# Turning the tests of an expert's rows, so that its arms stand short, middle, long in the program

## The chip, the cores and the metric

The kernel runs on one core of a Trainium2 chip. The metric is device time in microseconds (us), the median of three runs. The engines are PE (TensorE, matmuls; PEld is its weight load), DVE (VectorE), ACT (ScalarE), POOL (GpSimd) and SP (SyncE, which here issues the weight transfers). Each engine runs its own instruction stream, branches included.

## The reference, cut to what matters

Two transformer blocks are computed over 256 tokens of 1024 features. The first has a mixture of experts: 32 experts, each token goes to its four best. Cut from the reference:

```python
logits = (xt @ w_router).astype(jnp.float32) + b_router.astype(jnp.float32)
top_v, top_i = lax.top_k(logits, TOP_K)
gates = jax.nn.softmax(top_v, axis=-1)
...
def expert_block(args):
    xb, e = args
    hdn = xb @ w_gate_up[e] + b_gate_up[e]
    return clamped_swiglu(hdn) @ w_down[e] + b_down[e]
...
out = jnp.zeros((T, D), y.dtype).at[tok_sorted].add(y[dest] * g_sorted[:, None].astype(y.dtype))
```

How many tokens an expert gets is known only at run time. In these inputs 21 experts get up to 32, 8 get 33 to 64, and 3 get more.

## The kernel before

**Stages.** Up to about 201 us the kernel does the first block's attention and routing. From there to about 1195 us come the experts, and then the rest of the two blocks. All changes are in the experts' part.

**Weights.** Each expert has 12 slabs of 1 MB (eight of gate and up, four of down). The class Stream issues them on SP's queue (L192) into a ring of buffers, in the order in which they are used. A slab's buffer is free again when PE has done the last matmul that reads it; a transfer whose buffer isn't free waits on SP, and all later ones wait behind it.

**Arms.** For each expert the program holds several versions of the work, one for each class of row count n, and every engine branches to one of them: the few arm (n up to 32, functions few_up and few_down), the narrow arm (33 to 64, narrow_up and narrow_down) and the mid arm (over 64, mid_up and mid_down), with two wide passes ahead of it for more than 96 and 224 rows, which these inputs never take. An arm begins on PE with two bias matmuls (L1041), then come eight slabs of gate and up (L1028, with a weight tile of 128x32 in a few and 128x64 in a narrow arm; mid begins likewise but also gathers its rows, L1162), the preparation of the next expert's rows, and the down slabs (L1106 in few, L1036 in narrow, L1225 in mid). Its last step, rows_out, takes the result from PSUM into the tile Y with two copies on ACT (L1047) and two subtractions on DVE (L1050). Few and narrow arms read Y only at their middle, when combine adds the expert before; a mid arm needs DVE before its first matmul.

**The order of the arms.** The list of experts is unrolled: 32 times the tests, the long passes, mid, narrow, few, one behind the other, and then a join. The tests of an expert are L1344 (few or not), L1345 (narrow or not) and L1346 (wide or not). An arm that isn't last ends with a jump over the arms behind it to the join (shown at L1345 behind narrow); the last one runs on into the join. At the join PE loads the next count (L1324) and makes the next expert's tests. name_jump, at each arm's start, looks at the next expert's count (L1333) and gives PE a hint which of the next tests will be taken; the hint is an instruction of PE alone.

The times of the steps below are read from the trace. Experts are numbered from 0. The order that the counts give is: narrow 0, few 1, 2, narrow 3, 4, few 5, narrow 6, few 7, 8, mid 9, few 10, narrow 11, 12, mid 13, few 14 to 18, narrow 19, mid 20, few 21 to 24, narrow 25, few 26 to 31.

Of the kernel before, what the change touches and what calls it, by code (L numbers as in the profile page):

```python
# [96 lines left out]
def kernel(tc, a, out, taps=None, stop=None):  # L97
# [848 lines left out]
    def early_loads():  # L946
        nc.gpsimd.dma_start(gt_f, row(bt[1][:], D, 1024))
        load_gn(0)
        nc.gpsimd.dma_start(cols, a["cols"])
# [23 lines left out]
    def mask(e):  # L973
        for t in range(2):
            mask_rows(dm, t, e)
        slab_rows(e)
# [54 lines left out]
    def down(yb, hT, base, kk):  # L1031
        w = W.get(base + 8 + DS[kk // 2])
        j, c = divmod(kk, 4)
        for hf in range(2):
            o = (kk % 2) * 1024 + hf * 512
            nc.tensor.matmul(yb[64 * hf:64 * hf + 64, :], hT[:, c, j * 64:(j + 1) * 64], w[:, o:o + 512],  # L1036
                             start=(kk == KK[0]), stop=(kk == KK[-1]), skip_group_check=True,
                             tile_position=(0, 64 * hf))
# [13 lines left out]
    def combine(y, dT):  # L1052
        for t in range(2):
            for hf in range(2):
                nc.tensor.matmul(acc[t][:, hf * 512:hf * 512 + 512], dT[:, t, :], y[:, hf, :], start=False,
                                 stop=False, skip_group_check=True)
# [255 lines left out]
    def whole(up, down, e):  # L1312

        up(e)
        d = None
        if e:
            combine(Y, PRE[e - 1][1])
        if e + 1 < NE:
            mask(e + 1)
            d = dm  # L1320
        down(e, d, Y)

    def load_n(e):
        return nc.values_load(cnt[0:1, e:e + 1], min_val=0, max_val=T)  # L1324

    def name_jump(e, n):

        def likely(label):
            tc.mark_branch_hint_location(f"{label}{e}", "LikelyTaken", [mybir.EngineType.PE])

        if n is None:
            return
        with tc.If(n > 32) as c:  # L1333
            with tc.If(n > 64) as d:
                likely("wide")
            with d.Else():
                likely("narrow")
        with c.Else():
            likely("few")

    n = load_n(0)
    for e in range(NE):
        nn = load_n(e + 1) if e + 1 < NE else None
        with tc.If(n > 32, label=f"few{e}") as cmp:  # L1344
            with tc.If(n > 64, label=f"narrow{e}") as many:  # L1345
                with tc.If(n > 96, label=f"wide{e}"):  # L1346
                    wide(e, 96)
                    with tc.If(n > 224):
                        wide(e, 224)
                name_jump(e + 1, nn)  # L1350
                whole(mid_up, mid_down, e)
            with many.Else():
                name_jump(e + 1, nn)
                whole(narrow_up, narrow_down, e)
        with cmp.Else():
            name_jump(e + 1, nn)
            whole(few_up, few_down, e)
        for k in range(12):
            W.done(MOE0 + 12 * e + k)
        if e == 1:  # L1360
            early_loads()
        n = nn
# [606 lines left out]
```

## Time and profile before

| | before |
|---|---|
| median of three runs | 2091.35 us (2090.78 to 2092.16) |
| profiled execution, its own time | 2093.27 us |
| its span | 2091.5 us |
| mean granted clock of PE | 0.93 |
| PE busy | 1804.8 us (86%) |
| DVE, ACT, POOL busy | 45%, 32%, 18% |
| weights moved on SP's queue | 586.72 MB |

The span is what the trace covers; the profiled execution's time is 1.8 us longer. Shares over the whole span mix three stages. In the experts' part two things can set the pace: the stream of slabs, when PE sits waiting for a transfer, and PE, when the ring is full and the transfers wait for PE. Which of the two holds at a place is seen in the rate of the DMA engines there.

### The profile page before, as it was taken

To read this page: it belongs to the slowest core of one execution; us is meant where nothing else is said; L and a number is where in the kernel's file an instruction comes from. 1 tells how busy PE (TensorE), PEld (TensorE's weight loads), DVE (VectorE), ACT (ScalarE), POOL (GpSimd) and SP (SyncE) were. 2 spreads that over 40 slices of the span, in tenths; PEclk is the share of its full clock that TensorE was granted. 3 is DMA by queue.
4 is the path that set the end of the run, shared out by engine and by line. 5 is a ranking of instruction groups with operands and counts; after the bars stand their busy time and mean duration, and the time that the engine had idled before them with its cause. 6 is when DMAs were issued, how large, how long until landed. Compare 5 with 4: busy or idle time off the path is not lost.

```text
span 2091.5 us, 28801 instructions
## 1 busy us (share of the span) xinstructions
PE 1804.8 (86%) x11311; PEld 1159.1 (55%) x11311; DVE 943.7 (45%) x1687; ACT 674.8 (32%) x1149; POOL 366.6 (18%) x337
## 2 busy tenths in 40 slices
PE   7998898787897877797766688998999989999998
PEld 4775233222322222232221168997998778988996
DVE  3774222212212321131221259857575589665763
ACT  3452111101101110111110145544564456445752
POOL 3323000000000000000000044124352242132640
PEclk9997999998998989898988789999999999999999
DMA  9868999998968999899999853454455533453552
GB/s 399 348 244 305 407 418 418 419 418 357 419 273 331 417 419 418 349 376 420 417 419 418 347 196 109 142 183 171 155 188 213 178 133 134 162 201 131 182 198 84
DMA packets 85796, 602.35 MB, mean 288 GB/s; under 512 B 9888, under 2 KB 10576, under 8 KB 14256
## 3 DMA queue, kind: packets, MB, share of 16 engines
q1 hardware_dynamic: 81600, 586.72, 70.6%
q0 software_dynamic: 3952, 12.53, 2.0%
q8 instruction: 135, 2.21, 0.4%
q14 instruction: 109, 0.89, 0.1%
HBM read 598.13 MB, written 1.08 MB: 287 GB/s over the span
## 4 chain that ended last, share of the span: by engine, by line
issue 49%; PE 35%; DVE 10%; POOL 2%; ACT 2%; POOLq 1%; DVEq 0%; ACTq 0%
PE psum L354 11%; PE psum L353 10%; PE psum L352 10%; DVE lo L325 1%; DVE lx L325 1%; POOL v L245 1%; DVE gl L1740 1%; DVE gl L1524 1%; DVE h L577 1%; PE psum L1674 1%; DVE nm L570 1%; DVE x L285 0%; PE psum L448 0%; ACT hTh L357 0%; POOLq L1324 0%
## 5 line engine op out<-in xcount | busy, mean ns | idle before, releaser
L1028 PE MATMUL psum<-w,xT 128*32 128x512 f32 (+1 forms) x1504 | 268.6, 673 | 54.7 <-DMA w<-in_wgu_dram 52.6
L354 PE MATMUL psum<-hTh,lo 128*128 128x256 f32 x848 | 240.8, 284 | 2.9 <-DVE lo L325 2.9
L352 PE MATMUL psum<-hTh,hi 128*128 128x256 f32 x848 | 242.1, 286 | 0.4 <-DVE yl L1544 0.4
L353 PE MATMUL psum<-hTl,hi 128*128 128x256 f32 x848 | 240.6, 284 | 0.0
L248 POOL TENSOR_TENSOR yr<-v,mhalf 128x1 f32<-128x1 f32 (+1 forms) x26 | 21.0, 808 | 1146.6 <-DVE v L245 1145.3
L325 DVE TENSOR_TENSOR lo<-w,hi 128x2048 fp32r<-128x2048 f32 x84 | 193.7, 2309 | 59.3 <-ACT hi L319 59.3
L319 ACT ACTIVATE hi<-w 128x2048 fp32r<-128x2048 f32 x93 | 177.6, 1913 | 86.5 <-PE psum L354 51.2
L1028 PEld LDWEIGHTS psum<-w,xT 128*32 128x32 f32 (+1 forms) x1504 | 61.9, 125 | 238.7 <-issue 119.6
L1006 DVE TENSOR_SCALAR g<-psum 64x256 f32<-64x256 f32 (+1 forms) x70 | 29.3, 418 | 363.1 <-PE psum L1028 362.4
L1007 ACT ACTIVATE s<-g 64x256 f32<-64x256 f32 (+1 forms) x70 | 28.8, 411 | 474.9 <-DVE g L1006 474.9
L352 PEld LDWEIGHTS psum<-hTh,hi 128*128 128x128 f32 x848 | 162.6, 192 | 3.6 <-issue 2.9
L354 PEld LDWEIGHTS psum<-hTh,lo 128*128 128x128 f32 x848 | 162.5, 192 | 3.3 <-DVE lo L325 3.3
L353 PEld LDWEIGHTS psum<-hTl,hi 128*128 128x128 f32 x848 | 162.5, 192 | 0.0
L1050 DVE TENSOR_TENSOR y<-psum,y 64x512 fp32r<-64x512 f32 x64 | 44.1, 689 | 212.5 <-ACT y L1047 186.1
L1786 POOL TENSOR_TENSOR cv<-cv,cv 128x256 f32<-128x256 f32 x44 | 86.8, 1973 | 135.1 <-ACT cv L1785 135.1
L354 PE MATMUL psum<-hTh,lx 128*128 128x256 f32 x368 | 104.0, 283 | 2.9 <-DVE lx L325 2.9
L352 PE MATMUL psum<-hTh,hx 128*128 128x256 f32 x368 | 104.4, 284 | 0.0
L325 DVE TENSOR_TENSOR lx<-w,hx 128x2048 fp32r<-128x2048 f32 x40 | 92.4, 2310 | 26.3 <-ACT hx L319 26.2
L353 PE MATMUL psum<-hTl,hx 128*128 128x256 f32 x368 | 103.7, 282 | 0.0
L1041 PE MATMUL psum<-bgh,eb 128*128 128x512 f32 x70 | 30.3, 519 | 83.2 <-issue 73.6
L1780 DVE SCALAR_TENSOR_TENSOR cv<-psum,cols,cv 128x255 f32<-128x255 f32 x176 | 72.8, 476 | 61.9 <-ACT cv L1776 61.9
L319 ACT ACTIVATE hx<-w 128x2048 fp32r<-128x2048 f32 x43 | 82.3, 1913 | 38.5 <-PE psum L354 18.4
(427 smaller groups left out, 3759.6 us busy)
## 6 DMA issues: line engine op xcount, KB each, us to landing
w<-in_wgu_dram SPq DMA_DIRECT2D x169, 1024.0 KB, 19.8
w<-in_wpk_dram SPq DMA_DIRECT2D x168, 1024.0 KB, 4.9
w<-in_wd_dram SPq DMA_DIRECT2D x83, 1024.0 KB, 20.0
lo<-in_wgu_dram SPq DMA_DIRECT2D x29, 1024.0 KB, 19.8
hi<-in_wgu_dram SPq DMA_DIRECT2D x28, 1024.0 KB, 19.8
hi<-in_wd_dram SPq DMA_DIRECT2D x16, 1024.0 KB, 20.4
lo<-in_wd_dram SPq DMA_DIRECT2D x15, 1024.0 KB, 20.8
hx<-in_wgu_dram SPq DMA_DIRECT2D x15, 1024.0 KB, 19.9
```

The lines of the kernel that those rows point to most:

```text
L319: nc.scalar.activation(s.his[i], W.get(i), AF.Copy)
L325: (eng or nc.vector).tensor_tensor(s.los[i], W.get(i), s.his[i].bitcast(F32), OP.subtract)
L352: nc.tensor.matmul(o, lh, rh, start=start, stop=False, **k)
L353: nc.tensor.matmul(o, lh, rl, start=False, stop=False, **k)
L354: nc.tensor.matmul(o, ll, rh, start=False, stop=stop, **k)
L1006: nc.vector.tensor_scalar(g, gl[:, c], 7.0, None, op0=OP.min)
L1007: nc.scalar.activation(s, g, AF.Sigmoid, scale=1.702)
L1028: nc.tensor.matmul(b[o:o + n, :], l, w[:, q * 512:q * 512 + 512], start=False, stop=(k == 7), skip_group_check=True, tile_position=(0, o))
L1041: nc.tensor.matmul(b, lhsT, bgh[:, o:o + 512], start=first, stop=False, skip_group_check=True)
L1050: nc.vector.tensor_tensor(y[o, hf, :], yb[r, :], y[r, hf, :].bitcast(F32), OP.subtract)
L1780: nc.vector.scalar_tensor_tensor(cv[q][:, o], bnk[:, q, i], c4[q][:, 2 * d:2 * d + 1], cv[q][:, o], op0=OP.mult, op1=OP.add)
L1786: nc.gpsimd.tensor_tensor(cv[0], cv[0], cv[1], OP.mult)
```

## The change

Both inner tests are written the other way round, and their bodies exchanged with them: first the few arm, else the narrow arm, else the wide passes and mid. The argument preferred_fallthrough_block=False tells the compiler to lay the other body out behind the test, which keeps the long arm where it was.

```diff
--- before.py
+++ after.py
@@ -1341,20 +1341,20 @@
     n = load_n(0)
     for e in range(NE):
         nn = load_n(e + 1) if e + 1 < NE else None
-        with tc.If(n > 32, label=f"few{e}") as cmp:
-            with tc.If(n > 64, label=f"narrow{e}") as many:
+        with tc.If(n < 33, label=f"few{e}", preferred_fallthrough_block=False) as cmp:
+            name_jump(e + 1, nn)
+            whole(few_up, few_down, e)
+        with cmp.Else():
+            with tc.If(n < 65, label=f"narrow{e}", preferred_fallthrough_block=False) as many:
+                name_jump(e + 1, nn)
+                whole(narrow_up, narrow_down, e)
+            with many.Else():
                 with tc.If(n > 96, label=f"wide{e}"):
                     wide(e, 96)
                     with tc.If(n > 224):
                         wide(e, 224)
                 name_jump(e + 1, nn)
                 whole(mid_up, mid_down, e)
-            with many.Else():
-                name_jump(e + 1, nn)
-                whole(narrow_up, narrow_down, e)
-        with cmp.Else():
-            name_jump(e + 1, nn)
-            whole(few_up, few_down, e)
         for k in range(12):
             W.done(MOE0 + 12 * e + k)
         if e == 1:
```

In the built program the number of instructions, their waits and the semaphores are the same on each engine. The tests compare with 33 and 65 in place of 32 and 64, and are now at L1344, L1348 and L1352. Of the places in memory, mid's and the wide passes' are the same. Those of few and narrow are exchanged: in memory an expert's arms were mid, narrow, few, and are mid, few, narrow. On PE both have nearly the same number of instructions, so that the second place and the third are as large as before; only who stands there differs. The rows below are of PE, as the program lists its instructions. In it h is an expert's hidden rows, hT and the numbered xT tiles are the same transposed, xe the next expert's gathered rows, w a slab of weights, cst_85 a constant, and cnt the counts.

The end of the second place in expert 8, and what stands behind it, before:

```order
L998 MATMUL psum<-cst_85,xe 128x128 x4
L1036 MATMUL psum<-w,hT 64x512 x8
L1018 MATMUL psum<-cst_85,h 128x128 x2
L1036 MATMUL psum<-w,hT 64x512 x8
L1345 UNCONDITIONAL_BRANCH
L1333 COMPARE_AND_BRANCH
```

And after the change:

```order
L998 MATMUL psum<-cst_85,xe 128x128 x4
L1106 MATMUL psum<-w,xT_7924 32x512 x8
L1096 MATMUL psum<-cst_85,h 128x64 x2
L1106 MATMUL psum<-w,xT_7924 32x512 x8
L1344 UNCONDITIONAL_BRANCH
L1333 COMPARE_AND_BRANCH
```

The few arm (L1096 and L1106) now stands there, and it now has the end jump (L1344), over the arm behind it.

The end of the third place in expert 11, up to the tests of expert 12, before:

```order
L998 MATMUL psum<-cst_85,xe 128x128 x4
L1106 MATMUL psum<-w,xT_10815 32x512 x8
L1096 MATMUL psum<-cst_85,h 128x64 x2
L1106 MATMUL psum<-w,xT_10815 32x512 x8
L1344 UNCONDITIONAL_BRANCH
L1324 TENSOR_LOAD cnt
L1344 COMPARE_AND_BRANCH
L1345 COMPARE_AND_BRANCH
L1346 COMPARE_AND_BRANCH
```

And after:

```order
L998 MATMUL psum<-cst_85,xe 128x128 x4
L1036 MATMUL psum<-w,hT 64x512 x8
L1018 MATMUL psum<-cst_85,h 128x128 x2
L1036 MATMUL psum<-w,hT 64x512 x8
L1348 UNCONDITIONAL_BRANCH
L1324 TENSOR_LOAD cnt
L1344 COMPARE_AND_BRANCH
L1348 COMPARE_AND_BRANCH
L1352 COMPARE_AND_BRANCH
```

The narrow arm (L1018 and L1036) now stands last. The listing shows an end jump on each last arm; in the built program that jump leads to the next instruction and is left out, so that the last arm runs on into the load of the next count and the tests.

## Rows read from the trace of the kernel before

**Rows 1.** Busy time by stretch: us, five engines, PE clock, DMA share, GB/s.

```profile
605.00:670.00 65.00, 50.49 (x264) 16.43 (x266) 11.22 (x28) 5.83 (x13) 0.00 (x0) 0.84 0.61 231
...
895.00:1164.00 269.00, 206.62 (x1210) 64.55 (x1202) 64.26 (x169) 35.54 (x78) 0.00 (x0) 0.88 1.01 419
```

**Rows 2.** Timeline of PE, starts of arms: start, us, [idle before].

```profile
304.75 0.73 PE L1041 MATMUL psum<-bgh,eb 128*128 128x512 f32 x2 [2.94 <-issue]
...
391.19 1.22 PE L1041 MATMUL psum<-bgh,eb 128*128 128x512 f32 x2 [3.03 <-issue]
...
450.22 0.71 PE L1041 MATMUL psum<-bgh,eb 128*128 128x512 f32 x2 [3.00 <-DVEq L1346]
...
532.83 0.74 PE L1041 MATMUL psum<-bgh,eb 128*128 128x512 f32 x2
...
565.01 1.22 PE L1041 MATMUL psum<-bgh,eb 128*128 128x512 f32 x2 [4.31 <-issue]
...
597.77 0.70 PE L1041 MATMUL psum<-bgh,eb 128*128 128x512 f32 x2 [3.35 <-DVEq L1346]
...
664.01 1.21 PE L1041 MATMUL psum<-bgh,eb 128*128 128x512 f32 x2 [8.60 <-issue]
...
685.51 0.73 PE L1041 MATMUL psum<-bgh,eb 128*128 128x512 f32 x2 [2.50 <-issue]
...
702.90 0.73 PE L1041 MATMUL psum<-bgh,eb 128*128 128x512 f32 x2
...
721.12 0.73 PE L1041 MATMUL psum<-bgh,eb 128*128 128x512 f32 x2
...
757.64 1.22 PE L1041 MATMUL psum<-bgh,eb 128*128 128x512 f32 x2 [5.47 <-issue]
...
782.95 0.73 PE L1041 MATMUL psum<-bgh,eb 128*128 128x512 f32 x2
...
820.42 0.76 PE L1041 MATMUL psum<-bgh,eb 128*128 128x512 f32 x2 [3.24 <-DVEq L1346]
...
889.41 1.21 PE L1041 MATMUL psum<-bgh,eb 128*128 128x512 f32 x2 [8.85 <-issue]
...
1013.74 0.73 PE L1041 MATMUL psum<-bgh,eb 128*128 128x512 f32 x2 [2.90 <-issue]
```

**Rows 3.** Timeline of SP, its first issue behind the second middle arm.

```profile
667.15 0.33 SPq L192 DMA_DIRECT2D lx<-in_wgu_dram  x1
```

**Rows 4.** Branches in PE's sequencer, two lines: ns min/median/max, first and last start.

```profile
L1344 PEldq COMPARE_BRANCH  x32: 74/360/6084, 194.8 to 1162.3; - x32
...
L1346 PEldq COMPARE_BRANCH  x3: 346/5001/5160, 446.1 to 814.7; - x3
```

**Rows 5.** The same between 1005 and 1013.6 us: end jump, then the test.

```profile
L1345 PEldq COMPARE_BRANCH  x1: 335/335/335, 1007.2 to 1007.2; - x1
...
L1344 PEldq COMPARE_BRANCH  x1: 5251/5251/5251, 1008.1 to 1008.1; - x1
```

**Rows 6.** Timeline of DVE ahead of the first two middle arms.

```profile
448.61 1.41 DVE L1050 TENSOR_TENSOR y<-psum,y 64x512 fp32r<-64x512 f32 x2 [6.08 <-ACTq L1346]
...
595.76 1.41 DVE L1050 TENSOR_TENSOR y<-psum,y 64x512 fp32r<-64x512 f32 x2 [9.66 <-ACTq L1346]
```

**Rows 7.** Busy time by stretch, right behind five arm starts.

```profile
391.20:394.60 3.40, 3.40 (x18) 1.10 (x22) 1.28 (x5) 0.00 (x0) 0.00 (x0) 0.55 1.02 412
...
450.20:457.00 6.80, 6.78 (x43) 2.88 (x44) 1.81 (x7) 0.77 (x2) 0.00 (x0) 1.00 1.02 416
...
597.80:606.00 8.20, 8.20 (x38) 3.26 (x40) 1.59 (x7) 0.77 (x2) 0.00 (x0) 0.58 1.01 415
...
820.40:831.00 10.60, 8.80 (x36) 3.56 (x38) 1.75 (x7) 0.77 (x2) 0.00 (x0) 0.52 1.01 413
...
1013.70:1017.10 3.40, 3.36 (x30) 1.21 (x34) 0.00 (x0) 0.00 (x0) 0.00 (x0) 1.00 1.02 412
```

**Rows 8.** Timeline of PE in expert 19, its eighth slab.

```profile
801.99 1.94 PE L1028 MATMUL psum<-hx,xT 128*64 128x512 f32 x8 [0.55 <-DMA hx<-in_wgu_dram]
```


## The prediction

> **What bounds the kernel now.** I read the rates by stretch first. From 895 to 1164 us the transfers run at 419 GB/s with a DMA share of 1.01, so there the stream sets the pace; from 605 to 670 us they fall to 231 GB/s, since the ring is full and waits for PE [rows 1]. The transfers restart at 667.15 us [rows 3], 3.1 us after the few arm behind mid 13 starts at 664.01 [rows 2]; behind mid 20, whose few arm starts at 889.41, it is the same. After a restart the stream runs without a hole up to the next mid arm, and behind mid 20 to the end of the experts. So time lost by PE counts in two places: from the start of mid 9 (450.22) to the few arm at 664.01, and in mid 20, from 820.42 to 889.41. Elsewhere a few arm that doesn't wait takes 702.90 to 721.12, 18.2 us [rows 2], and its 12 slabs of 1.05 MB each take 30 us at 419 GB/s, so some 5 us more hide behind the stream.
>
> Then I read the starts of arms with the idle time ahead of each [rows 2]. Starts behind few are mostly without a gap (532.83, 702.90, 721.12, 782.95); starts behind narrow have 2.90 to 4.31 us. The reason stands in PE's own branches. Behind narrow 25 the end jump takes 0.335 us, and then the test of the next expert takes 5.25 us [rows 5]. This is so behind each of the eight narrow arms (5.00 to 5.46). Behind few the test takes about 0.36 us, the median of the line, in 13 of 20 cases, and 3.1 to 6.1 us in the other seven [rows 4]. The test starts about 1 to 2.5 us ahead of the last matmul's end, since PE's sequencer runs ahead of its queue, and so 5.2 us of test give some 3 to 5 us of gap. I read it thus: the test jumps over the arms ahead of its target, PE has to fetch the code there, and the hint at an arm's start starts that fetch early. Behind the last place, which runs on into the test, the early fetch is still there mostly; behind the second place, whose jump passes over a whole arm, it is not.
>
> The Trainium skill bears on this ("Runtime: NRT & Kernel Launch", Instruction fetch mechanics): prefetch is purely sequential, and a taken branch out of the two pages held has to fetch its target first. By it all far tests would stall, whichever place an arm has, and the change would give nothing. The trace doesn't agree: 13 tests behind few are short [rows 4], in a kernel with hints.
>
> **The change part by part.** The instructions, waits and semaphores are the same, and the tests' other constants cost nothing. What moves is who stands in the second place (jump over one arm) and who in the third (runs on). I take the cost to go with the place, since the jump and the distance belong to it: 20 exits from few with a successor get the full stall, and most of the eight exits from narrow lose it. Most of that hides. On the path are these, in order.
>
> 1. *Few 8 to mid 9.* Before, its test took 0.346 us, the smallest of its line [rows 4], and the gap is 3.00 [rows 2], because mid waits for DVE, which ends at 448.61 + 1.41 = 450.02 [rows 6], 0.2 us ahead of the start. With jump and stall PE's branches end later than that: the gap becomes that of a full stall behind few, 0.33 + 5.1 less the 1.1 us by which the test starts ahead of the matmuls' end, plus 0.7 from test to matmul, so 5.0 (bounds from rows: 4.31 and 5.47). That is +2.0. Behind it the clock, too: right behind the start at 450.22 it is granted 1.00 (2.4 GHz), but behind mids that start after 3.35 and 3.24 us of gap 0.58 over 8.2 us and 0.52 over 10.6 us, which is mostly the lower level, 1.2 GHz [rows 7]. A gap of 5.0 brings that: 8.2 x 0.42 = 3.4 or 10.6 x 0.48 = 5.1, taken +4.3. Sum **+6.3** (+4.7 to +7.6).
> 2. *Few 10 to narrow 11.* Gap 0 at 532.83, then 5.05: +5.05. A narrow arm that starts after a long gap costs more by its clock: 565.01 to 597.77 less the gap of 3.35 is 29.4, 532.83 to 565.01 less 4.31 is 27.9 [rows 2], so +1.5. Sum **+6.6** (+5.8 to +7.0).
> 3. *Narrow 11 to narrow 12.* Narrow now runs on into the test: gap 4.31 to 0, and the slow start goes: **-5.8**.
> 4. *Narrow 12 to mid 13.* The test falls from 5.16 to 0.35, but DVE holds the start: it ends at 595.76 + 1.41 = 597.17 [rows 6], 0.6 us ahead of the start at 597.77, where 0.2 would do. So -0.4, and the gap becomes 2.95. The open question is the clock. Behind narrow a gap of 2.90 kept it at 1.00 and one of 3.03 had 0.55 [rows 2, 7]; behind few 3.00 kept it. I give it a bit less than even odds to stay up, and enter 45% of the 3.4: -1.5. Sum **-1.9** (-3.8 to -0.4).
> 5. *Narrow 19 and mid 20.* Few 14 to 17 get stalls: two starts without gap become 5.05 each, that at 685.51 grows by 2.5, and each loses some 1.5 by the clock, 17 in all. Few 17 lasts 36.5 with a gap of 5.47, 12.8 more than 18.2, and few 18 25.3, 7 more, all of it waiting for slabs; these take it up. Narrow 19 then starts 5.05 later than 782.95, at 788.0. Its eighth slab starts at 801.99 after a wait for its transfer [rows 8]; now 788.0 + 0.7 + 7 x 1.94 + 1.5 for the clock = 803.8, so +1.8. Mid 20's start gains 0.3 as in 4, and its clock 0 to 5.1, taken 45%: -2.3. Sum **-0.8** (-3.6 to +1.5).
>
> The other stalls and gains fall where the stream sets the pace, at nil: few 2, 5 and 7 ahead of mid 9, few 21 to 30 behind mid 20. Without that cover each would cost 5 to 6.5. The last expert's arm has no next test; its jump costs 0.3 and the last combine waits longer for Y. The jump out of mid, and the test behind it, stay as they are.
>
> Together +6.3 + 6.6 - 5.8 - 1.9 - 0.8 = **+4.4 us**. The profiled execution took 2093.27, 1.9 above the median; the sum of differences is put on the median, 2091.35, which gives 2095.7.
>
> **The rivals.**
> - *Clock as before* or *clock won twice.* The same mechanism with the two open clocks at their ends: both mids start slowly again, 2.3 + 1.5 more than the sum, 2099.5; both start at full clock, 2.8 + 1.9 less, 2091.0. Both are within the forecast's case and make its range.
> - *Narrow stalls in the third place, too.* Seven of 20 exits from there did. If narrow 11's does, term 3 goes (+5.8) and the time is about 2101.5. Against it: the narrow arm lasts 28 us to few's 18 with as many instructions, so an early fetch has more time. It decides at one exit.
> - *The stall goes with the arm.* If narrow stalls since of what it does, or few's short test has another reason than its place, or the code lies as before for PE, nothing moves: 2091.4. For it: eight of eight against 13 of 20 is also a split by arm. Against it: seven exits of few stall at times as long, and both arms carry the same hint.
> - *Every far test stalls, whatever its place.* The short tests behind few would then be the odd ones, and no place worse than another: each exit as before, 2091.4. The rule of the Trainium skill named above is this case. Against it the 13 short tests [rows 4]; 0.03.
> - *Few does not stall behind its jump, though narrow loses its stall.* Terms 1 and 2 vanish, and 5's +1.8: -5.8 - 1.9 - 0.3 - 2.3 = -10.3, 2081.1. The faster side. For it: few reaches its jump sooner after its hint, so that what the hint fetched may not yet be displaced. Against it: the jump's target lies as far away as narrow's did.
>
> **How the numbers follow.** A measurement of this kernel tells about 0.2%, 4.2 us, from no change: faster is below 2087.2, slower above 2095.5. The forecast's mechanism has 0.73: with both clocks low 0.22 (2099.5), one low 0.36 (2096.1 with 13's won, 2094.4 with 20's won), both full 0.15 (2091.0). Narrow's stall staying has 0.10 (2101.5), the arm's stall or nothing moved 0.09 (2091.4), every far test alike 0.03 (2091.4), few without a stall 0.05 (2081.1). Slower: 0.22, two thirds of 0.36's first half, a quarter of its second, and most of 0.10, together 0.48. Faster: 0.05 and a little of the case with both clocks full, 0.07. The rest, 0.45, is no change to be told. The range leaves out the case without few's stall and the upper part of narrow's: 2089.5 to 2101.0. The forecast, 2095.7, lies at the edge of what can be told, and slower is the likelier side by little.
>
> **What would show it.** In the profile after, the starts behind few should have gaps near 5 (narrow 11, narrow 19, mid 9), with PE's test behind each few arm at 5.0 to 5.5 and an end jump of about 0.33; the start of narrow 12 should have none, and the mids at 13 and 20 a gap of 2.9 to 3.0 with the test at 0.35. The few arm behind mid 13 should start some 5 later counted from mid 9's place, and the transfers restart 3.1 behind it. Stalls should stand at about 26 of 31 exits, where there were 18. The step is wrong if the tests behind few stay short, if the test behind narrow 11 is long, or if the clock behind mid 9's start stays at 1.00.

## The result, and the profile after

The changed kernel takes 2109.47 us, the median of four runs (2101.28 to 2117.04), against 2091.76 for the kernel before (2090.78 to 2093.32). The ratio is 1.0081 with an interval of 1.0064 to 1.0098: slower by 17.7 us of the medians, less than 1% but clear of the noise. The forecast was 2095.7 with a range up to 2101.0, so the direction was the one held likelier, and the size that was forecast is four times too small, with the time outside the range. The profiled execution took 2101.28, the fastest of the four; a second trace, below, is of a longer one.

These are the starts of arms in the profiled execution, on PE, with the idle time ahead of each in brackets. They answer to [rows 2]; the views are of short windows, which cut a line's duration and count.

```profile
451.96 0.79 PE L1041 MATMUL psum<-bgh,eb 128*128 128x512 f32 x2 [4.96 <-DVE d L1155]
...
543.69 0.80 PE L1041 MATMUL psum<-bgh,eb 128*128 128x512 f32 x1 [5.19 <-issue]
...
573.53 0.73 PE L1041 MATMUL psum<-bgh,eb 128*128 128x512 f32 x2
...
604.35 0.71 PE L1041 MATMUL psum<-bgh,eb 128*128 128x512 f32 x2 [2.95 <-DVEq L1352]
...
667.85 0.79 PE L1041 MATMUL psum<-bgh,eb 128*128 128x512 f32 x1 [9.01 <-issue]
...
695.18 0.79 PE L1041 MATMUL psum<-bgh,eb 128*128 128x512 f32 x1 [8.49 <-issue]
...
718.70 0.79 PE L1041 MATMUL psum<-bgh,eb 128*128 128x512 f32 x1 [4.67 <-issue]
...
742.43 0.69 PE L1041 MATMUL psum<-bgh,eb 128*128 128x512 f32 x1 [4.70 <-issue]
...
775.29 0.80 PE L1041 MATMUL psum<-bgh,eb 128*128 128x512 f32 x1 [10.86 <-issue]
...
803.03 0.79 PE L1041 MATMUL psum<-bgh,eb 128*128 128x512 f32 x1 [7.99 <-issue]
...
835.92 0.70 PE L1041 MATMUL psum<-bgh,eb 128*128 128x512 f32 x2 [2.95 <-DVEq L1352]
```

Mid 9, narrow 11, narrow 12 and mid 13 (the first four) have the gaps that were forecast: 5.0, 5.05, none and 2.95. The few arm behind mid 13 starts 3.8 later than before, where the sum to there was +5.2. What was not forecast are the gaps of 8 to 11 us at 695.18, 775.29 and 803.03, which is behind few 14, few 17 and few 18.

The branches of PE show why. These are the branches at L1344 (end jump of a few arm, and the test for a few arm) and L1348 (test for a narrow arm), in the columns of [rows 4]. The first row is from the end of few 14, with jump and test on one line, the second of few 17 likewise. The third is few 18 (the jump, and a test not taken) and the last two few 10.

```profile
L1344 PEldq COMPARE_BRANCH  x2: 4088/4706/5324, 684.8 to 689.4; - x2
...
L1344 PEldq COMPARE_BRANCH  x2: 5476/5700/5924, 762.6 to 769.0; - x2
...
L1344 PEldq COMPARE_BRANCH  x2: 84/1630/3176, 793.2 to 796.8; - x2
...
L1344 PEldq COMPARE_BRANCH  x2: 84/202/319, 536.6 to 537.4; - x2
L1348 PEldq COMPARE_BRANCH  x1: 5282/5282/5282, 537.6 to 537.6; - x1
```

Behind few 10 it is as forecast: the jump 0.319, the test 5.28. Behind few 14 the jump alone takes 4.09 us, and the test 5.32 on top; behind few 17 the jump takes 5.92 and the test 5.48; behind few 18 the jump takes 3.18. Nine of the 20 exits from few have such a long jump (few 1, 7, 14, 17, 18, 21, 24, 27, 28: 2.9 to 6.1 us), the other eleven have 0.32 to 0.35. Seven of the nine are the very experts whose test was long behind the third place before; the other two, 18 and 28, had a short one.

The granted clock behind the starts of mids 9, 13 and 20, in the columns of [rows 7]:

```profile
452.00:460.00 8.00, 8.00 (x36) 3.22 (x38) 1.33 (x5) 0.54 (x2) 0.00 (x0) 0.57 1.02 418
...
604.30:611.10 6.80, 6.75 (x43) 2.87 (x44) 1.82 (x7) 0.77 (x2) 0.00 (x0) 1.00 1.01 414
835.90:842.70 6.80, 6.78 (x43) 2.90 (x44) 1.81 (x7) 0.77 (x2) 0.00 (x0) 1.00 1.01 413
```

Mid 9 lost its full clock, as forecast, and in this execution mids 13 and 20 both won theirs. The starts on the path, in us from the span's start, for all kernels of this study. The first expert's arm starts at 200.7 to 204.5 in these traces, so that differences within a row tell more than the starts themselves.

| kernel | mid 9 | few 14 | narrow 19 | mid 20 | few 21 | few 14 to narrow 19 |
|---|---|---|---|---|---|---|
| before | 450.2 | 664.0 | 783.0 | 820.4 | 889.4 | 118.9 |
| after | 452.0 | 667.9 | 803.0 | 835.9 | 900.3 | 135.2 |
| after, second trace | 453.6 | 666.6 | 807.3 | 840.5 | 908.5 | 140.7 |
| after, arms laid out early | 453.6 | 672.4 | 796.3 | 829.7 | 897.5 | 123.9 |
| before, arms laid out early | 451.1 | 667.7 | 787.0 | 824.7 | 890.5 | 119.3 |
| after, 14 to 18 in the old order | 454.5 | 674.4 | 794.7 | 831.4 | 894.6 | 120.4 |
| after, early, 8 and 10 in the old order | 452.3 | 658.5 | 782.6 | 816.2 | 881.6 | 124.1 |
| before without hints | 468.5 | 698.2 | 822.0 | 856.4 | 923.1 | 123.8 |
| after, arms laid out late | 486.5 | 727.1 | 879.2 | 913.8 | 983.6 | 152.2 |

In the profiled execution the loss behind few 14 stands in one stretch: from there to narrow 19 it is 16.2 us, of which 4.6 come back in narrow 19, which waited for slabs before, and 4.6 in mid 20 by its clock. So few 21 starts 10.9 later, and the rest of the experts, paced by the slabs, follows: the first matmul behind them starts at 1218.79 where it was 1206.82. Of these 12.0 us 4.0 come back behind the experts, in code that didn't change (why isn't shown), and this execution is 8.0 longer than the profiled one before.

### The profile page after: what moved, and what is told of

It is laid out like the page before. It is cut to its first block, busy times and chain, and to the rows that moved or that the text cites. A ratio compares the mean times of both kernels' runs of the same rounds, so it can differ in the third digit from the quotient of the medians.

```text
span 2099.5 us, 28866 instructions
## 1 busy us (share of the span) xinstructions
PE 1781.8 (85%) x11311; PEld 1159.7 (55%) x11311; DVE 944.3 (45%) x1687; ACT 674.8 (32%) x1149; POOL 366.7 (17%) x337
## 4 chain that ended last, share of the span: by engine, by line
issue 50%; PE 34%; DVE 10%; ACT 2%; POOL 2%; POOLq 1%; DVEq 0%; ACTq 0%
PE psum L354 10%; PE psum L353 10%; PE psum L352 10%; DVE lo L325 1%; DVE lx L325 1%; POOL v L245 1%; DVE gl L1740 1%; DVE h L577 1%; DVE gl L1524 1%; DVE nm L570 1%; DVE x L285 0%; PE psum L1674 0%; ACT hTh L357 0%; POOLq L1324 0%; PE psum L448 0%
## 5 line engine op out<-in xcount | busy, mean ns | idle before, releaser
L1028 PE MATMUL psum<-w,xT 128*32 128x512 f32 (+1 forms) x1504 | 258.1, 660 | 16.3 <-DMA w<-in_wgu_dram 10.6
L1041 PE MATMUL psum<-bgh,eb 128*128 128x512 f32 x70 | 36.7, 618 | 168.8 <-issue 157.9
L1041 PEld LDWEIGHTS psum<-bgh,eb 128*128 128x128 f32 x70 | 15.0, 267 | 199.5 <-issue 199.5
## 6 DMA issues: line engine op xcount, KB each, us to landing
w<-in_wgu_dram SPq DMA_DIRECT2D x169, 1024.0 KB, 19.8
hi<-in_wgu_dram SPq DMA_DIRECT2D x28, 1024.0 KB, 19.8
```

What stands on the lines that cost most here:

```text
L1028: nc.tensor.matmul(b[o:o + n, :], l, w[:, q * 512:q * 512 + 512], start=False, stop=(k == 7), skip_group_check=True, tile_position=(0, o))
L1041: nc.tensor.matmul(b, lhsT, bgh[:, o:o + 512], start=first, stop=False, skip_group_check=True)
```

## The experiments

**The changed kernel once more.** No edit; more executions and a second trace.

> The changed kernel once more, for the spread of its times and for a second trace. Theory J (an end jump of a few arm that now stands second stalls for 3 to 6 us when it comes soon after PE has begun a new piece of code, on top of the 5.3 us of the test): the same nine exits, from few 1, 7, 14, 17, 18, 21, 24, 27 and 28, have gaps of 7 to 11 us again, the other eleven 4.3 to 5.3. Theory C (the spread of the four times, 2101 to 2117, is the clock behind the starts of mids 13 and 20, 3.4 and 5.1 us, which the first trace has at full): in a run some 8 us longer than the first, mids 13 and 20 last 66 and 69 us in place of 63.5 and 64.4, and the few arms start where they did. Rival R: another set of jumps stalls in each run; then the gaps differ. Median 2105 to 2112.

Measured: 2107.85 us (2100.16 to 2112.73), ratio 1.0065 (1.0042 to 1.0087). The same nine jumps are long in this trace, each within 0.3 us of the first; rival R falls. Theory C is right only in part. The execution's span is 2110.9, 11.4 longer; mid 20 takes 68.0 us, 3.6 more than in the first trace, but mid 13 takes even less than there. Few 17 takes 3.1 more, and 2.5 were lost before the first expert. In few 17 the clock differs, behind a gap of 4.6 here and 4.7 there. The first trace, over the 10.2 us behind the start of few 17, in the columns of [rows 7]:

```profile
742.40:752.60 10.20, 7.93 (x53) 2.13 (x57) 0.42 (x1) 0.00 (x0) 0.00 (x0) 0.83 1.01 414
```

And the second trace, over as much:

```profile
743.00:753.20 10.20, 8.06 (x29) 1.82 (x33) 0.42 (x1) 0.00 (x0) 0.00 (x0) 0.50 1.01 413
```

The lower of the two levels lasts through all of the 10.2 us in the second, and for about a third of it in the first (0.83 on average). So a part of the spread comes from the clock behind gaps, which came back sooner in one trace than in the other, and there are now more of these gaps on the path. The same holds of mid 20: behind a gap of 2.95 in both traces, it was granted 1.00 in the first and 0.50 in the second. What decides how long the clock stays down isn't shown, and the rest of the spread isn't accounted for.

**The arms laid out so that no jump is long.** Instructions are put where they never run, in the second wide pass, so that the code of each expert from 2 on becomes 7 x 256 instructions long on PE:

```diff
+    def pad(e):
+        b = bank("gl")
+        for _ in range({0: 0, 1: 26}.get(e, 91)):
+            nc.tensor.transpose(b[:, 0:128], ident, ident)
...
                     with tc.If(n > 224):
                         wide(e, 224)
+                        pad(e)
```

> The changed kernel with 52 transposes' worth of PE instructions in expert 1's and 182 in each later expert's second wide pass, which never runs here, so that each expert's code on PE is 7 x 256 instructions long and each arm lies as expert 19's does, whose neighbours 15, 22 and 26 have an unstalled jump. Theory J: no end jump of a few arm is longer than 0.4 us from expert 2 on, the tests behind it stay at 5.0 to 5.7, gaps 4.3 to 5.3. Then few 14 starts as in the changed kernel, some 4 us later than in the kernel before, but narrow 19 is reached without the 12 us of stalled jumps between: 2092 to 2098 if the mids start at full clock, up to 2102 with both at half. Rival (the stalled jumps have nothing to do with where the code lies): nine stalled jumps, 2101 to 2112.

Measured: 2097.69 us (2090.25 to 2101.33), ratio 1.0025 (1.0012 to 1.0038). The end of few 14, jump and test, in this kernel (the jump is the smaller number):

```profile
L1349 PEldq COMPARE_BRANCH  x2: 319/3110/5902, 689.4 to 690.3; - x2
```

And the start of few 15 behind it:

```profile
696.66 0.78 PE L1041 MATMUL psum<-bgh,eb 128*128 128x512 f32 x1 [5.38 <-issue]
```

The jump falls from 4.09 to 0.32, the gap from 8.49 to 5.38, and so at all exits from expert 2 on. With the jumps short, the time is 5.5 above the median of before in the same batch (2092.2), where the prediction's sum was +4.4. Its parts stand too: few 14 to narrow 19 is 4.9 longer than before (term 5 had 5.05), mid 9 to few 14 is 5.0 longer, with mid 13 partly at the lower clock (0.61 over 6.8 us).

**The kernel before with the same filling.** The edit is the same, on the kernel before.

> The kernel before with the same filling in the wide passes that never run. Theory J: the seven long tests behind a few arm in the third place (3.1 to 6.1 us) become 0.35 too, since all third places now lie as expert 26's does; the eight behind narrow stay at 5.0 to 5.5. Six of the seven lie where the slabs set the pace, one (few 14 to 15) behind a mid: time within 3 us of the kernel before. Rival: the seven stay.

Measured: 2091.07 us (2083.97 to 2095.26), ratio 0.9997 (0.9984 to 1.0010). The test behind few 14, in the third place, in the kernel before:

```profile
L1344 PEldq COMPARE_BRANCH  x1: 3487/3487/3487, 681.6 to 681.6; - x1
```

And in this one:

```profile
L1349 PEldq COMPARE_BRANCH  x1: 347/347/347, 685.4 to 685.4; - x1
```

All seven are short now (0.34 to 0.37), the eight behind narrow as long as before. It changes no time: those stalls were hidden. But it shows that the long tests behind the third place and the long jumps behind the second go with one thing, where the arm's code lies on PE.

**Only experts 14 to 18 in the old order.** The rest is the changed kernel.

```diff
+        if 14 <= e <= 18:
+            with tc.If(n > 32, label=f"few{e}") as cmp:
...
+        else:
+            with tc.If(n < 33, label=f"few{e}", preferred_fallthrough_block=False) as cmp:
```

> The changed kernel, but experts 14 to 18 keep the order of before (mid, narrow, few). If the loss beyond the forecast lies in the few arms between mid 13 and narrow 19, whose five exits then run on as before, narrow 19 and mid 20 start where few 14's start puts them, 156 to 157 us behind it as before (168 in the changed kernel), and the time falls by 8 to 12 us against the changed kernel: 2092 to 2100, depending on the mids' clocks. Rival (the loss is elsewhere, or spread): no change or a few us, 2101 to 2110.

Measured: 2096.12 us (2090.18 to 2100.59), ratio 1.0014 (1.0001 to 1.0027): about 12 us below the changed kernel by medians. The starts of few 14 and narrow 19:

```profile
674.37 0.79 PE L1041 MATMUL psum<-bgh,eb 128*128 128x512 f32 x1 [9.69 <-issue]
...
794.73 0.73 PE L1041 MATMUL psum<-bgh,eb 128*128 128x512 f32 x2
```

From one to the other it takes 120.4 again, and from few 14 to mid 20 it is 157.0 (before 156.4). So the loss beyond the forecast lies in these five exits.

**Experts 8 and 10 in the old order, arms laid out early.** The edit is that of the run before, with `e in (8, 10)`, together with the filling.

> As after_paged, but experts 8 and 10 keep the order of before, so that their few arms stand third and run on into the tests. Theory of the prediction (terms 1 and 2 are on the path): mid 9 starts with a gap of 3.0 at full clock, narrow 11 without a gap, narrow 12 without a gap; from mid 9's start to few 14's is 203 to 208 us (before 213.8, after_paged 218.8 with mid 13 at half clock), and the time is 10 to 13 us below after_paged: 2084 to 2088. Rival (what PE loses there is hidden by the slabs): within 3 us of after_paged, 2095 to 2100.

Measured: 2083.57 us (2081.6 to 2086.17), ratio 0.9962 (0.9948 to 0.9977), 14.1 below the same kernel with all experts turned (by medians of two batches), a little more than expected. The starts of mid 9, narrow 11, narrow 12 and mid 13:

```profile
452.27 0.71 PE L1041 MATMUL psum<-bgh,eb 128*128 128x512 f32 x2 [3.00 <-DVEq L1374]
...
536.37 0.73 PE L1041 MATMUL psum<-bgh,eb 128*128 128x512 f32 x2
...
564.15 0.73 PE L1041 MATMUL psum<-bgh,eb 128*128 128x512 f32 x2
...
594.96 0.71 PE L1041 MATMUL psum<-bgh,eb 128*128 128x512 f32 x2 [2.95 <-DVEq L1374]
```

Terms 1 and 2 were 12.9 together; undoing them gives 14.1, and from mid 9 to few 14 takes 206.3 in place of 218.8. Of these 12.5 us 3.1 are mid 13, which ran at full clock here and not there and belongs to neither term, so that the good match of the sum is in part luck. This kernel is the fastest of all here (0.4% below the kernel before), but it knows beforehand which experts are few: with other counts other exits are on the path.

**The kernel before without hints.**

```diff
     def name_jump(e, n):
...
-        if n is None:
-            return
+        return
```

> The kernel before without the hints and the tests that choose them (name_jump left empty). Theory H (the hint at an arm's start is why the test behind the third place is short): every test behind few takes 5.0 to 5.7 us, as behind narrow, gaps 4 to 5; on the path few 8 to mid 9 (+6), few 10 to narrow 11 (+6.5), and narrow 19 a bit later: 2102 to 2108. Rival (the place alone does it, the code behind an arm that runs on is there anyway): 13 short tests remain, 2089 to 2094.

Measured: 2122.81 us (2121.46 to 2123.65), ratio 1.0148 (1.0130 to 1.0167). The tests for few, narrow and wide, in the columns of [rows 4]:

```profile
L1343 PEldq COMPARE_BRANCH  x32: 82/6026/7812, 197.2 to 1195.7; - x32
...
L1345 PEldq COMPARE_BRANCH  x3: 6066/6546/6832, 462.1 to 849.5; - x3
```

No test that is taken is short any more: the median of the first line goes from 0.36 to 6.03, and each of the 31 exits has a gap of 4.2 us or more. Theory H holds: the hint is what makes the third place good. (Without the hint's instructions the code also lies elsewhere, which was not held fixed; but the stall stands at all 31 exits, wherever they lie.) The time is 15 to 21 above what was expected: 14.7 us are lost ahead of mid 9, where the expectation took the slabs to hide everything; 31 gaps are more than the waits for slabs there could take up.

**All experts laid out as the worst one.** Filling of 188 in place of 52 instructions in expert 1.

```diff
-        for _ in range({0: 0, 1: 26}.get(e, 91)):
+        for _ in range({0: 0, 1: 94}.get(e, 91)):
```

> As after_paged, but with 188 instead of 52 instructions in expert 1's wide pass, so that every later expert's code lies as expert 7's does in the changed kernel, whose end jump took 6.08 us. Theory J: every few arm's end jump from expert 2 on takes 5 to 6.5 us and its test 5.0 to 5.7, gaps 9 to 11.5. On the path: mid 9 and narrow 11 start some 6 later each, and the chain few 14 to narrow 19, five exits of 10.5 in place of 5, is PE's alone: 2125 to 2140. Rival (the stalled jumps were an accident of those nine experts): 2095 to 2112.

Measured: 2203.26 us (2199.45 to 2205.38), ratio 1.0532 (1.0508 to 1.0556). The end of few 15, jump and test:

```profile
L1349 PEldq COMPARE_BRANCH  x2: 5472/5809/6146, 775.0 to 781.6; - x2
```

And the start of narrow 19, behind few 18:

```profile
879.22 0.79 PE L1041 MATMUL psum<-bgh,eb 128*128 128x512 f32 x1 [10.83 <-issue]
```

The jumps are long everywhere, and 136 instructions more of code that never runs, in one expert, make 106 us of difference. The expected 2125 to 2140 was far too low. Narrow is hit in the third place as well: seven of its eight tests take 6.0 to 7.3 us here, with gaps of 3.4 to 4.6, which the expectation left out. And with some 10 us at each few exit PE no longer keeps up with the slabs anywhere (no matmul of the experts waits for one): from the experts' start to mid 9 it takes 283.0 us where the other layout takes 250.7.

## Why the prediction was wrong, point by point

- **The bound and the path** held ahead of few 14 and in mid 20: time counted there, and it came through the starts that were named. Undoing two exits in 8 and 10 moved the time by about what they were priced at. Between few 14 and narrow 19, which the prediction gave to the slabs, they did not hold (term 5).
- **The stall goes with the place: right.** All 20 exits from few have a test of 5.0 to 5.8 us, where 13 were short; the eight from narrow have 1.34 at most, where all were 5.0 or more. The rivals that the stall goes with the arm, that nothing moves, that narrow stalls in the third place, and that few doesn't stall behind its jump, all fall. But narrow was spared by where its experts lie: in the last experiment seven of its eight tests stall in the third place.
- **Term 1** (+6.3): the gap and the start are right (4.96, +1.7). The clock was granted 0.57 over 8.0 us, 3.4 us by the way of reckoning of the forecast, and the arm lasts 2.5 longer: 4.2 in all, so some 2 too high.
- **Terms 2 and 3**: narrow 11 has 5.19 ahead of it and narrow 12 nothing, as said. Narrow 12 to mid 13 shrinks by 1.9. Few 10 itself lasts 1.5 longer beyond the gap, which no term had. So terms 2 and 3 were some 2 too low, and that mid 13 starts 6.6 later, where the terms give 6.7, is in part luck.
- **Term 4**: DVE holds mid 13's start at 2.95, as said. Its clock, entered at 45%, was won in both traces of the changed kernel, and partly lost in the one with the filling.
- **Term 5 failed**, and in it one number: the end jump of few at 0.33 us, taken from [rows 5]. Behind few 14, 17 and 18 it measured 4.09, 5.92 and 3.18, 13.2 us in all, 12.2 more than three jumps of 0.33. The term was -0.8; the profiled execution gives +7.0 (16.2 - 4.6 - 4.6) and the second trace +16.5 (21.8 - 4.3 - 1.0). The waits for slabs in few 17 and 18 were to take up 17 us of stalls. The matmuls' waits for slabs that the profile shows there, in the kernel before, come to less than the 19.8 that the prediction took for waiting (line, what is waited for, us in all, times, longest; 721.1 to 782.9 us):

```profile
PE psum L1028 <- DMA w<-in_wgu_dram: 11.7, 10, 2.3
```

In the kernel with the filling, whose jumps are short, few 14 to 16 last 16.8 longer than before and few 17 and 18 give about that much back, as forecast. But that was all there was to give: from few 14 to few 21 no matmul waits for a slab any more, there or in the changed kernel. So nothing was left to hide the 12.2 us, and nearly all of them came through, 16.2 against 4.9 from few 14 to narrow 19.

- **What the rows had told.** Seven tests behind few in the third place were long, up to 6.08 us [rows 4]. The prediction counted them as a risk for narrow's test, and not for few's jump, though few was to leave from a place with the same size. All eight jumps of narrow were short or nearly so (0.31 to 1.77), but none of the eight is among the nine experts whose place is bad for few, so they couldn't tell. The longest two were signs all the same: 1.57 behind narrow 11, inside the gap of 4.31 that the prediction took as a bound, and 1.77 behind narrow 4, with a gap of 4.92 that its "2.90 to 4.31" leaves out. The same two experts have narrow's longest tests after the change (0.97 and 1.34). For two rivals the prediction weighed narrow's 28 us against few's 18, each time as a gain; that the longer arm is safer was not shown, and in the last experiment narrow's tests are long too.
- **The spread** was not forecast. The kernel before lies within 2087 to 2098 over the batches here, the changed one within 2100 to 2117. More gaps on PE's path are followed by more stretches at 1.2 GHz, and in the two traces these last a different time (few 17, mid 20); two traces can't show that this is all of it.
- **By the rule of the Trainium skill** ("Runtime: NRT & Kernel Launch", Instruction fetch mechanics), a taken branch to code that isn't held waits for it. The runs agree with that for the tests behind an arm in the kernel without hints (5.7 to 7.8 us at L1343 to L1345 when taken), and don't agree with "Prefetch is purely sequential": with hints 20 of 20 tests behind few in the third place take about 0.35 us once the code is laid out for it.

## What to carry to other kernels

In a program like this one, with hints, the arm that runs most belongs last, where it runs on into the next tests; an arm that leaves by a jump paid 5.0 us or more for the next far test here, in spite of the hint. Read such stalls with the place of the code: the same jump cost 0.3 or 6 us here, by where the arm lay on PE, and code that never runs can move it. Before a stall is called hidden, add up all that the same cover would have to hide, and look at every branch at the exit for its worst case elsewhere in the trace, not for its usual one.

## What the runs showed of the hardware

A long branch of PE is a wait for code. The code comes in pieces of one size on a queue of its own (q8), 2.21 MB in 135 packets before, which is 16.4 KB each. From 195 to 1300 us of the changed kernel's trace PE has 35 branches of over 2.5 us; within each of them one such piece lands, 1.3 to 1.6 us before the branch ends, and none lands within the 82 branches of under 0.5 us. This is the queue (packets, MB, share) during the long jump of few 14, from 684.8 to 688.9:

```profile
q8 instruction: 1, 0.02, 1.6%
```

During the short jump of few 15 (712.1 to 712.6) nothing moves on it. Why a piece is there in time for one jump and not for another, beyond that it goes with where the code lies, isn't shown. This is the line for the whole span, of the kernel before:

```profile
q8 instruction: 135, 2.21, 0.4%
```

Of the changed one:

```profile
q8 instruction: 150, 2.46, 0.5%
```

Of the one without hints:

```profile
q8 instruction: 165, 2.70, 0.5%
```

The changed kernel, with the same instructions, fetched 15 pieces more, and the one without hints 30; that pieces were fetched twice fits this, but isn't shown. Their number alone doesn't set the time: the kernels with short and with long jumps by filling fetched 149 each. That a layout alone is worth 106 us (2097.69 against 2203.26), and that a hint is worth 31 (2091.3 against 2122.81), was not expected. There are stalls within an arm as well: few 17 of the changed kernel stops for 2.24 us between two matmuls early in the arm, with no wait that the trace shows.

```profile
747.63 0.63 PE L1028 MATMUL psum<-w,xT 128*32 128x512 f32 x4 [2.24 <-issue]
```

A piece of code lands in this stop too, 1.4 us before its end, as in the long branches. The queue from 745 to 747.6:

```profile
q8 instruction: 1, 0.02, 2.6%
```

The second trace has the same stop (2.14 us) with a piece in it.
